# Seven products instead of eight in part of a down projection, and an FFN ordered by a list scheduler

## The chip, the cores and the metric

The kernel runs on one core of a Trainium2 chip. The metric is the device time of one execution in microseconds (us), taken as the median over runs of the same program. The engines are named as in the profile: PE (TensorE) multiplies matrices into eight banks of PSUM, PEld loads its stationary operand, DVE (VectorE) and ACT (ScalarE) do elementwise work and copy banks out, POOL (GpSimd) and SP (SyncE) issue transfers. ACT can issue transfers too.

## The reference

One decoder block on 256 tokens of width 2048, all in float32: a conditioning vector gives six shift, scale and gate vectors (adaLN); a mixed layer (attention and a gated short convolution) comes first; the FFN that the change is about comes last. Cut to that part:

```python
mod = silu(c) @ w_ada + b_ada
sh1, sc1, g1, sh2, sc2, g2 = split(mod, 6)
...
x  = x + g1 * (mixed @ w_out)
h2 = modulate(rms_norm(x, norm2_g), sh2, sc2)
u  = causal_dwconv(h2 @ w_ffn_up, ffn_conv_w, ffn_conv_b)   # 3 taps along the tokens, per channel
u_gate, u_up = split(u, 2)                                  # 5632 channels each
x  = x + g2 * ((silu(u_gate) * u_up) @ w_ffn_down)          # 5632 -> 2048
```

## The kernel before

**Precision.** Each float32 operand `t` of a product is split in two parts for PE: `hi` (ACT copies `t` to the type float32r, L266) and `lo = t - hi` (DVE subtracts, L272). A product is three matmuls: hi by hi, hi by lo, lo by hi. So each loaded weight tile (128 partitions x 4 k-chunks x 512 columns, 1 MB) costs ACT one copy and DVE one subtraction of 128x2048 before PE can use it. Tiles come in six `raw` buffers, `hi` and `lo` have three buffers each. A load starts when `split_lo` has freed a `raw` buffer.

**Slots.** All weight work from the input projection on is one list `slots`; each slot is one weight tile: its load on SP's queue, its split, and a function `go` that issues its matmuls. The main loop walks the list; in turn `i` it issues the split of slot `i + 2` and the matmuls of slot `i`, and between them the small work that `at(i, f)` has put down for that turn. The order on each engine is thus written out by hand: `CFG` holds lags in slots (`up0`, `up`, `gate`, `back`, `slag`, `hi_late` and others), and each engine works through its queue in that order.

**FFN up.** 22 groups of 256 channels. A tile holds 256 gate columns and the 256 up columns that belong to them, loaded as two transfers of 512 KB (L252). Weights are stationary here, the 256 tokens move: per 128x128 block one matmul of 512 columns (tokens' hi and lo side by side, L875) and one of 256 (weight's lo, L878). A group takes four slots (16 k-chunks) and four banks. Six groups are begun on the first eight k-chunks, two slots each (12 slots, called half-turns below), while the rest of the second norm's output is being made, four of them in a form that writes 256 columns only (L861). Then `up_sum` copies the banks out on ACT and adds on DVE, `up_conv` does the three taps (ACT the first with the bias, L734, DVE the two others, L739), `up_silu` and `up_gate` form the gated value and its hi and lo parts `gh`, `gl`.

**FFN down.** The 22 groups are taken in four segments (8, 5, 5 and 4 groups). After a segment's up projection its part of the down projection runs: four column blocks `f` of 512; tokens are stationary (two halves of 128) and weights move, 512 columns per matmul; per k-chunk and `f` there are 2 token halves x 3 matmuls (L433 to L435). Two banks collect a segment for one `f`. `evac_down` sums the segments in eight tiles `dacc` in SBUF. In the last segment `gate_down` multiplies `dacc` by the gate g2 and adds x, which had been parked in the output tensor (`spill`, `unspill`); the last column block has g2 multiplied into its weights instead (L264, `fold`).

**adaLN for g2.** Sixteen tiles of `w_ada` are loaded among the slots and summed on DVE (L330), then spread over the partitions by PE (`spread`).

Of the kernel before, what the change touches and what calls it, by code (L numbers as in the profile page):

```python
# [14 lines left out]
P = 128  # L15
D = 2048
S = 256
# [43 lines left out]
 'slag': [6, 21],  # L61
 'sgap': [2, 6],
# [5 lines left out]
 'up': [[0, 0, 1], [1, 3, 3], [0, 0, 1], [0, 3, 3]],  # L68
 'gate': [-16, -17, -6, -9],
# [17 lines left out]
         'up_conv': 2,  # L87
         'att_p': 0,
# [10 lines left out]
         'gate_down': -1,  # L99
         'conv_g': 2,  # L100
# [9 lines left out]
 'up0': [[0, 2, 4], [0, 3, 3], [0, 2, 2], [0, 1, 2], [2, 2, 4], [2, 4, 6], [0, 1, 2], [0, 0, 5], [3, 4, 4],  # L110
         [0, 2, 3]],
# [5 lines left out]
 'back': [-28, -26, -15, -19],  # L117
# [4 lines left out]
 'hi_late': [5, 8, 12, 14, 15, 16, 17, 18, 19, 20, 21, 23, 27, 28, 35, 39, 40, 45, 49, 53, 56, 58, 61, 65, 66, 67,  # L122
# [12 lines left out]
def tile_block(  # L135
# [11 lines left out]
    sb = ctx.enter_context(tc.tile_pool(name="sb", bufs=1))  # L147
    ps = ctx.enter_context(tc.tile_pool(name="ps", bufs=1, space=bass.MemoryType.PSUM))
# [78 lines left out]

    def load_next():
        if pending:
# [5 lines left out]
            pending.pop(0)(t)  # L235
            ready.append(t)

    def take():
        t = ready.pop(0)
        return t  # L240
# [19 lines left out]
    def split_hi(nk, gate=None):  # L260
        t = take()
        if gate is not None:
            w = t[:, :nk]
            V.tensor_tensor(out=w, in0=w, in1=gB[gate].unsqueeze(1).to_broadcast([P, nk, 512]), op=ALU.mult)  # L264
        hi = sb.tile([P, 4, 512], F32R, tag="hi", bufs=N_HL, name="hi")
        act(hi[:, :nk], t[:, :nk], AF.Copy)  # L266
        halfway.append((t, hi, nk))

    def split_lo():
        t, hi, nk = halfway.pop(0)  # L270
        lo = sb.tile([P, 4, 512], F32R, tag="lo", bufs=N_HL, name="lo")
        V.tensor_tensor(out=lo[:, :nk], in0=t[:, :nk], in1=hi[:, :nk].bitcast(F32), op=ALU.subtract)  # L272
# [11 lines left out]
    class Ada:  # L284
# [30 lines left out]
        def consume(self, r):  # L315
            t = self.view(take())
# [435 lines left out]
    def up_sum(grp, one):  # L752

        new = grp not in ub
        if one:
            if new:
                ub[grp] = [t2k(f"ub{grp}") for _ in range(2)]
            for ft in range(4):
                p, d = zp[grp][ft][:, :256], ub[grp][ft // 2][:, (ft % 2) * 256:(ft % 2) * 256 + 256]
                if new:  # L760
                    act(d, p, AF.Copy)
                else:
                    V.tensor_tensor(out=d, in0=p, in1=d, op=ALU.add)
            del zp[grp]
            return
        c = [t2k(f"ub{grp}") for _ in range(2)]
        for ft in range(4):
            act(c[ft // 2][:, (ft % 2) * 256:(ft % 2) * 256 + 256], zp[grp][ft][:, 256:], AF.Copy)  # L768
# [3 lines left out]
        if new:  # L772
            ub[grp] = c
        else:
            for a, b in zip(ub[grp], c):
                V.tensor_tensor(out=a, in0=a, in1=b, op=ALU.add)
        del zp[grp]

    def up_conv(grp):
        uy[grp] = [t2k(f"uy{grp}") for _ in range(2)]  # L780
        for w in range(2):
            conv3(ub[grp][w], uy[grp][w], fcols[:3], fcols[3], w * 44 + 2 * grp, CFG["taps"][1] if grp < CFG["taps"][2] else 0)
        del ub[grp]

    def up_silu(grp):
        act(uy[grp][0], uy[grp][0], AF.Silu)

    def up_gate(grp):
        g, u = uy.pop(grp)
        V.tensor_tensor(out=g, in0=g, in1=u, op=ALU.mult)  # L790
        hi, lo = t2k(f"gh{grp}", F32R), t2k(f"gl{grp}", F32R)
        act(hi, g, AF.Copy)  # L792
        V.tensor_tensor(out=lo, in0=g, in1=hi.bitcast(F32), op=ALU.subtract)  # L793
# [6 lines left out]
    def fold(seg, f):  # L800
        return seg == len(SEGS) - 1 and f >= CFG["fold"]

    def evac_down(seg, f):
        assert seg < len(SEGS) - 1 or f"gd{f}" in done
        done.add(f"ed{seg}{f}")
        for t in range(2):
            p = mainp["D", seg, f][t]
            if seg == 0:
                dacc[t, f] = t2k(f"da{t}{f}")
                act(dacc[t, f], p, AF.Copy)  # L810
            elif seg < len(SEGS) - 1:
                V.tensor_tensor(out=dacc[t, f], in0=p, in1=dacc[t, f], op=ALU.add)
            else:
                y = t2k(f"d{f}{t}")
                w = 256 if f == 3 and t == 1 else 512
                for h in range(0, 512, w):
                    s = slice(h, h + w)
                    p = mainp["D", seg, f][t + h // 256]
                    if fold(seg, f):
                        V.tensor_tensor(out=y[:, s], in0=p[:, :w], in1=x1[t, f][:, s], op=ALU.add)  # L820
                    else:
                        V.tensor_tensor(out=y[:, s], in0=p[:, :w], in1=gB[G2, f][:, s], op=ALU.mult)
                        V.tensor_tensor(out=y[:, s], in0=y[:, s], in1=x1[t, f][:, s], op=ALU.add)
                    nc.sync.dma_start(rows_of(t, f)[:, s], y[:, s])

    def gate_down(f):
        assert f"ed{len(SEGS) - 2}{f}" in done
# [4 lines left out]

    SEGS, a = [], 0
    for n in CFG["segs"]:
        SEGS.append((a, a + n))
        a += n

    NS, *cut = CFG["split"]
    for seg, (ga, gb_) in enumerate(SEGS):
        turns = [((0, 16), range(ga, gb_))]  # L840
        if seg == 0:
            turns = [(ks, range(NS)) for ks in zip([0] + cut, cut + [16])] + [((0, 16), range(NS, gb_))]
        for n, (ks, grps) in enumerate(turns):
            for grp in grps:
                if seg == 0 and n < len(cut) + 1 and grp < CFG["direct"][min(n, 1)]:
                    direct.setdefault(grp, []).append(ks)
                for k in range(ks[0], ks[1], 4):
                    def go(hi, lo, grp=grp, k=k, ks=ks):
                        if k == ks[0]:
                            zp[grp] = [bank(f"z{grp}_{ft}") for ft in range(4)]  # L850

                        order = [(j, ft) for j in range(4) for ft in range(4)]
                        begins, ends = k == ks[0], k + 4 == ks[1]
                        if grp in direct and ks in direct[grp]:
                            for j in range(4):
                                for ft in range(4):
                                    o, a = zp[grp][ft][:, :256], slice(ft * P, (ft + 1) * P)
                                    for w, v in ((hi, 0), (hi, 1), (lo, 0)):  # L860
# [12 lines left out]
                        for j, ft, w in run:
# [529 lines left out]
```

## Time and profile before

| | before |
|---|---|
| median of 3 runs | 1173.9 us (1173.8 to 1174.57) |
| span of the profiled execution | 1170.4 us |
| PE busy | 1151.1 us |
| DVE busy | 921.9 us |
| ACT busy | 626.3 us |
| POOL busy | 12.0 us |
| moved by DMA | 318.00 MB, mean 272 GB/s |

The three runs shown lie between 1173.8 and 1174.57 us; the profiled execution is told by its span, from the first to the last instruction, 3.5 us under the median of the runs. Busy is the time in which an engine has at least one instruction at work. A matmul's own duration overlaps that of the next, so the pace of matmuls is read from the starts of two that lie far apart. The trace can be cut into stretches: for each, the busy time of every engine, and the matmul clock that the chip granted.

### The profile page before, as it was taken

Reading aid. Unit: us, or ns where it says so; the run is one execution under the profiler, and the core shown is the slowest. Engines: PE = TensorE matmul, PEld = TensorE weight load, DVE = VectorE, ACT = ScalarE, POOL = GpSimd, SP = SyncE. Lnnn points to the kernel's source line nnn. Section 1 sums busy time; section 2 is a strip of 40 time slices with the busy share of each in tenths; the row PEclk is TensorE's granted clock in tenths of the full one; section 3 lists DMA queues with packets and bytes.
Section 4 is the critical chain, followed back from the end, with each engine's and each line's share of the span. In section 5 each row is a group of like instructions: output and inputs, shape, how many; then the busy total and the mean of one; then the engine's idle time right before and its main releaser. Section 6 shows DMA issues by size and latency. Waiting matters only on the chain.

```text
span 1170.4 us, 15668 instructions
## 1 busy us (share of the span) xinstructions
PE 1151.1 (98%) x6115; PEld 973.6 (83%) x6115; DVE 921.9 (79%) x1030; ACT 626.3 (54%) x906; POOL 12.0 (1%) x24
## 2 busy tenths in 40 slices
PE   5999999999999999999999999999999999999998
PEld 3777778888888889988888888888888888888886
DVE  3889989999999978899876767986556576478766
ACT  6645365567785564666664444555444554336441
POOL 1000000000000000000000000000000000000000
PEclk9999999999999999999999999999999999999999
DMA  9999989999899799975555898984664646675441
GB/s 364 406 415 411 409 321 372 378 349 347 287 332 350 251 326 331 359 253 178 186 194 168 305 337 301 310 279 154 208 222 159 201 162 216 222 252 168 150 162 73
DMA packets 189052, 318.00 MB, mean 272 GB/s; under 512 B 7073, under 2 KB 105845, under 8 KB 184625
## 3 DMA queue, kind: packets, MB, share of 16 engines
q1 hardware_dynamic: 187232, 314.60, 75.6%
q10 hardware_dynamic: 1296, 2.16, 0.5%
q8 instruction: 48, 0.79, 0.3%
q0 software_dynamic: 448, 0.24, 0.1%
q14 instruction: 28, 0.22, 0.1%
HBM read 312.77 MB, written 4.19 MB: 271 GB/s over the span
## 4 chain that ended last, share of the span: by engine, by line
PE 91%; DVE 3%; ACT 2%; DMA 2%; issue 1%; SPq 0%; DVEq 0%; ACTq 0%
PE z L875 24%; PE z L878 13%; PE z L861 4%; DVE lo L272 1%; PE ada L324 1%; PE mk L443 1%; PE mk L444 1%; PE mk L441 1%; PE mq L443 1%; PE mq L444 1%; PE mq L441 1%; PE mx L443 1%; PE mc L443 1%; PE mx L444 1%; PE mc L444 1%; PE mv L443 1%
## 5 line engine op out<-in xcount | busy, mean ns | idle before, releaser
L272 DVE TENSOR_TENSOR lo<-raw,hi 128x2048 fp32r<-128x2048 f32 (+2 forms) x201 | 445.9, 2224 | 140.4 <-ACT hi L266 135.5
L266 ACT ACTIVATE hi<-raw 128x2048 fp32r<-128x2048 f32 (+2 forms) x201 | 373.8, 1865 | 311.9 <-PE z L875 60.2
L875 PE MATMUL z<-h,hi 128*128 128x512 f32 x1280 | 299.0, 390 | 0.2 <-DVE h L696 0.2
L875 PEld LDWEIGHTS z<-h,hi 128*128 128x128 f32 x1280 | 237.6, 188 | 48.1 <-PE z L875 0.6
L330 DVE SCALAR_TENSOR_TENSOR ada<-raw,csil,ada 128x512 f32<-128x512 f32 (+3 forms) x167 | 195.4, 1175 | 5.6 <-DMA raw<-in_w_ada_dram 2.1
L878 PEld LDWEIGHTS z<-h,lo 128*128 128x128 f32 x1280 | 159.3, 192 | 3.4
L878 PE MATMUL z<-h,lo 128*128 128x256 f32 x1280 | 160.5, 283 | 0.0
L739 DVE SCALAR_TENSOR_TENSOR uy<-ub,fc,uy 128x254 f32<-128x254 f32 (+1 forms) x176 | 71.3, 476 | 0.2
L771 DVE TENSOR_TENSOR ub<-z,ub 128x256 f32<-128x256 f32 x96 | 33.9, 415 | 37.9 <-ACT ub L768 37.9
L792 ACT ACTIVATE gh<-uy 128x512 fp32r<-128x512 f32 x22 | 13.9, 632 | 62.9 <-DVE uy L790 62.9
L861 PE MATMUL z<-h,hi 128*128 128x256 f32 x256 | 46.6, 284 | 0.4 <-ACT h L693 0.2
L734 ACT ACTIVATE uy<-ub,fc,fc 128x256 f32<-128x256 f32 x88 | 45.6, 602 | 0.0
L768 ACT ACTIVATE ub<-z 128x256 f32<-128x256 f32 x96 | 28.8, 384 | 31.4 <-PE z L875 31.4
L861 PEld LDWEIGHTS z<-h,hi 128*128 128x128 f32 x256 | 40.0, 192 | 0.8 <-ACT h L693 0.5
L861 PE MATMUL z<-h,lo 128*128 128x256 f32 x128 | 36.2, 283 | 0.0
L324 PE MATMUL ada<-raw,crep 128*32 128x256 f32 (+1 forms) x192 | 20.3, 535 | 7.9 <-DMA raw<-in_w_ada_dram 7.9
L793 DVE TENSOR_TENSOR gl<-uy,gh 128x512 fp32r<-128x512 f32 x22 | 15.2, 692 | 15.4 <-ACT gh L792 15.4
L443 PE MATMUL mq<-hi,h 128*128 128x512 f32 x64 | 25.5, 398 | 0.4 <-DVE adaz L361 0.4
L443 PE MATMUL mx<-hi,h 128*128 128x512 f32 x64 | 25.7, 401 | 0.0
L443 PE MATMUL mc<-hi,h 128*128 128x512 f32 x64 | 25.6, 400 | 0.0
L443 PE MATMUL mk<-hi,h 128*128 128x512 f32 x64 | 25.1, 393 | 0.0
L443 PE MATMUL mv<-hi,h 128*128 128x512 f32 x64 | 25.1, 392 | 0.0
(612 smaller groups left out, 1885.4 us busy)
## 6 DMA issues: line engine op xcount, KB each, us to landing
raw<-in_w_ada_dram SPq DMA_DIRECT2D x96, 1024.0 KB, 6.8
raw<-in_w_ffn_up_dram SPq DMA_DIRECT2D x176, 512.0 KB, 4.5
raw<-in_w_in_dram SPq DMA_DIRECT2D x47, 1024.0 KB, 7.8
raw<-in_w_ffn_down_dram SPq DMA_DIRECT2D x28, 1024.0 KB, 5.0
raw<-in_w_out_dram SPq DMA_DIRECT2D x16, 1024.0 KB, 6.0
raw<-in_w_ffn_down_dram SPq DMA_DIRECT2D x20, 768.0 KB, 4.2
xr<-in_x_dram SPq DMA_DIRECT2D x2, 1024.0 KB, 6.4
x<-in_x_dram SPq DMA_DIRECT2D x8, 256.0 KB, 6.6
```

What stands on the lines that cost most here:

```text
L266: act(hi[:, :nk], t[:, :nk], AF.Copy)
L272: V.tensor_tensor(out=lo[:, :nk], in0=t[:, :nk], in1=hi[:, :nk].bitcast(F32), op=ALU.subtract)
L324: mm(self.acc[q:q + 32, :], crep[:, i, :], t[:, j, :], start=(r == 0 and j < 4), stop=(r == self.tiles - 1 and j >= self.rows - 4), tile_p ...
L330: V.scalar_tensor_tensor(out=self.acc, in0=t[:, j, :], scalar=csil[:, i:i + 1], in1=self.acc, op0=ALU.mult, op1=ALU.add)
L443: mm(o, a, hi[:, k, s], start=(first and k == 0), stop=False)
L444: mm(o, b, hi[:, k, s], start=False, stop=False)
L734: act(y[:, s], b[:, s], AF.Identity, bias=bias[:, i + j:i + j + 1], scale=w[2][:, i + j:i + j + 1])
L739: V.scalar_tensor_tensor(out=o[:, d:], in0=v[:, :256 - d], scalar=w[2 - d][:, i + j:i + j + 1], in1=o[:, d:], op0=ALU.mult, op1=ALU.add)
L771: V.tensor_tensor(out=d, in0=zp[grp][ft][:, :256], in1=d, op=ALU.add)
L861: mm(o, w[:, j, a], h2T[k + j][:, v * 256:v * 256 + 256], start=begins and j == 0 and w is hi and not v, stop=ends and j == 3 and w is lo)
L875: mm(zp[grp][ft], hi[:, j, ft * P:(ft + 1) * P], h2T[k + j], start=begins and j == 0, stop=ends and j == 3)
L878: mm(zp[grp][ft][:, :256], lo[:, j, ft * P:(ft + 1) * P], h2T[k + j][:, :256], start=False, stop=False)
```

## The change

It touches the FFN alone, from the first half-turns of the up projection to the end.

1. **Seven products.** Six groups (three in segment 0, two in 1, one in 2; segments are now 8, 6, 4 and 4 groups) are multiplied in the down projection by a Strassen-Winograd scheme. A block is 2 token halves by 2 k-chunks, times 2 k-chunks by 2 column blocks: eight products of 128x128 by 128x512 become seven, each still three matmuls. It needs sums of weights (`sums_of`, three DVE instructions, made in place in the `raw` tile) and sums of tokens (`st_sums`, `st_hi`, `st_lo`). Such a group and column pair takes two slots: `r` (three products, straight from the loaded tile) and `T` (four products, split from the sums, no load of its own). The other groups (`c`) keep eight.
2. **Eight banks and a detour.** Two column blocks are done together, so that a segment and column pair collects in eight banks: four of plain results and four partial products (`a`, `5`, `6`, `7`). `evac_q` copies each out on ACT and POOL adds it to a tensor in DRAM by an accumulating transfer. At the end `load_q` brings the 16 sums back and `join` adds them on DVE. `dacc` and its adds go.
3. **Up projection by half.** A unit is 512 columns of the gate half or of the up half, one transfer of 1 MB, instead of 256 and 256. Two units make two groups. The taps move to ACT: two more scaled copies for each (`utaps` 2), DVE only adds them.
4. **List scheduler.** From the slot after the half-turns on, every piece of work is an `Op` with an engine, a planned cost, what it depends on, a due time and the buffers it needs; a greedy loop emits the piece that can start first, by due time. Every fourth `hi` and `lo` tile now comes from the `raw` buffers, which makes them four deep and leaves four `raw` buffers for loads.
5. **End.** The last segment runs its column blocks in another order (`tail`), with block 3 in the last two slots. Blocks 0 and 1 are added to the output in DRAM by accumulating transfers, blocks 2 and 3 get x by an accumulating transfer into SBUF. The loads for g2 move to the units 9 to 17.

```diff
- 'segs': [8, 5, 5, 4],
+ 'plan': [6, 0, 1, 7, 2, 3, 8, 4, 5, 9, (0, 0), (0, 1), 10, 11, 12, 13, 14, 15, (1, 0), (1, 1), 16, 17, 18, 19, (2, 1), (2, 0), 20, 21],
+ 'tail': [(0,36,4),(1,36,4),(2,36,4),(0,40,4),(1,40,4),(2,40,4),(3,36,4),(3,40,4)],
+ 'utaps': 2,
+ 'segs': [8, 6, 4, 4],
+ 'forms': ['cScScScc', 'cScScc', 'cScc'],
...
+    def half_tile(tag, i):
+        t, n = (tag, N_HL) if i < DEEP or (i - DEEP) % 4 else ("raw", N_RAW)
...
+    def sums_of(t):
+            V.tensor_tensor(out=t[:, 1::2], in0=t[:, 1:3], in1=t[:, 3:4].to_broadcast([P, 2, 512]), op=ALU.add)
+            V.tensor_tensor(out=t[:, 2], in0=t[:, 2], in1=t[:, 1], op=ALU.add)
+            V.tensor_tensor(out=t[:, 0], in0=t[:, 0], in1=t[:, 2], op=ALU.add)
...
+        for d in range(CFG["utaps"] + 1):
+            for j in range(2):
+                if d:
+                    act(z[d - 1][:, s], ub[unit][w][:, s], AF.Copy, scale=fcols[2 - d][:, i:i + 1])
+                else:
+                    act(y[:, s], ub[unit][w][:, s], AF.Identity, bias=fcols[3][:, i:i + 1], scale=fcols[2][:, i:i + 1])
...
+    def evac_q(seg, fp, n):
+            e = t2k(f"e{fp}{n}")
+            act(e, qb.pop((seg, fp, n)), AF.Copy, scale=-1.0 if n in ("a", "c00", "c10") else 1.0)
+            if (fp, n) in qd:
+                nc.gpsimd.dma_start(qd[fp, n], e, accum_op=ALU.add)
+            else:
+                qd[fp, n] = dram.tile([P, 512], F32, name=f"q{fp}{n}")
+                nc.gpsimd.dma_start(qd[fp, n], e)
...
+            if e == "c":
+                todo.append(("c", [(f"c{t}{f}", (tok, j, t), 2 * j + f) for f in range(2) for t in range(2) for j in range(2)], g))
+            else:
+                todo.append(("r", [("a", (tok, *a11), 2), ("c00", (tok, *a12), 0), ("c01", (sT, g, 3), 1)], g))
+                todo.append(("T", [("c10", (tok, *a22), 0), ("7", (sT, g, 1), 1), ("6", (sT, g, 2), 2), ("5", (sT, g, 0), 3)], g))
...
+                    mm(qb[seg, fp, n], y, hi[:, b], start=first[n] == (i, j), stop=False)
+                    mm(qb[seg, fp, n], x, hi[:, b], start=False, stop=False)
+                    mm(qb[seg, fp, n], x, lo[:, b], start=False, stop=last[n] == (i, j))
...
+        for j in ([j] if j < len(slots) else []):
+            d = [pe.get(j - 4)]
+            if kind.get(j) == "T":
+                d.append(sum_op[j - 1])
+            hi_op[j] = prev["hi"] = Op("ACT", 1.81 * nk / 4 + 0.02, lambda j=j: split_hi(slots[j][1], gated.get(j), j), d, key=raw)
+            lo_op[j] = prev["lo"] = Op("DVE", 2.2 * nk / 4 + 0.03, lambda j=j: split_lo(j), [hi_op[j]])
+            if kind.get(j) == "r":
+                sum_op[j] = Op("DVE", 2.4, lambda j=j: sums_of(held[j]), [lo_op[j]])
```

More of the change, by code (lines that the diff above doesn't have):

```diff
@@ L234, in load_next, with arrive, take @@
             t = sb.tile([P, 4, 512], F32, tag="raw", bufs=N_RAW, name="raw")
[L235 to L240, printed above, removed]
+            issue = pending.pop(0)
+            issue(t)
+            ready.append((issue, t))
+            if clock:
+                arrive(issue)
+    clock, landed = {}, {}
+    def arrive(issue):
+        clock["DMA"] = max(clock["DMA"], clock["now"] + 1.5) + 2.7
+        landed[issue] = clock["DMA"] + 1.5
+    def take(issue=None):
+        for e in ready:
+            if issue in (None, e[0]):
+                ready.remove(e)
+                return e[1]
     def w_load(w, k0, nk, cols):
@@ L833, in tile_block @@
+    NS, *cut = CFG["split"]
     SEGS, a = [], 0
@@ L1342, in tile_block, with hi_of, lo_of @@
     at(CFG["vload"] + CFG["fcols"], ffn_cols)
[L1345 to L1347 removed]
+    def hi_of(js):
+        for j in js:
+            split_hi(slots[j][1], gated.get(j), j)
+    def lo_of(js):
+        for j in js:
+            split_lo()
+    for i in range(F0):
+        js = from_(i)
+        if i == F0 - 3:
+            skip.extend((0, 0))
         last = i in CFG["x_first"]
[L1349 to L1350 removed]
+        late = [j for j in js if i == N_OUT or i in CFG["hi_late"]]
+        if not last:
+            hi_of([j for j in js if j not in late])
         now[0] = i
@@ L1355, in tile_block @@
                 f(*a)
-        if more and hi_late and not last:
-            split_hi(slots[i + LA][1], gated.get(i + LA))
-        if more and not last:
-            split_lo()
+        if not last:
+            hi_of(late)
+            lo_of(js)
         for c, f, a in todo:
@@ L1366, in tile_block, with __init__ @@
             g.consume(r)
-        if more and last:
-            split_hi(slots[i + LA][1], gated.get(i + LA))
-            split_lo()
+        if last:
+            for j in js:
+                hi_of([j])
+                lo_of([j])
+    clock.update(PE=0.0, ACT=0.0, DVE=0.0, SP=0.0, POOL=0.0, DMA=0.0, now=0.0)
+    ops = []
+    class Op:
+        def __init__(self, e, cost, f, deps=(), due=1e9, need=(), free=(), lat=0.1, key=None, out=0, nb=0.0):
+            self.e, self.cost, self.f, self.deps, self.due = e, cost, f, [d for d in deps if d], due
+            self.need, self.free, self.lat, self.end, self.key = dict(need), dict(free), lat, None, key
+            self.out, self.nb = out, nb
+            ops.append(self)
@@ new lines, in tile_block, with up_ops @@
+    prev = {}
+    spread_at = {[i for i, g in up_slots if g == e][k]: j for j, (e, k) in enumerate(CFG["spread"])}
+    def up_ops(i):
+        for grp, one, final in ups_at.get(i, []):
+            a = Op("ACT", 1.06, lambda grp=grp, one=one: up_sum_a(grp, one), [pe.get(i)], need={"t": 2}, free={"b": 4} if one else {})
+            if not one:
+                merge = grp in started and final
+                a = Op("DVE", 1.33 + (1.22 if merge else 0), lambda grp=grp: up_sum_v(grp), [a, done_1.get(grp)],
+                       free={"b": 4, "t": 2 if merge else 0})
+            if not final:
+                done_1[grp] = a
+            freeing.append((i, a, 4))
+            if final:
+                chain(grp, a)
@@ new lines, in tile_block, with run_slot @@
+    free = 8
+    q = list(freeing)
+    for i in range(F0, len(slots)):
+        while free < slots[i][4] and q:
+            _, a, n = q.pop(0)
+            a.due = min(a.due, tid[i])
+            free += n
+        free -= slots[i][4]
+    for o in reversed(ops):
+        for d in o.deps:
+            d.due = min(d.due, o.due - o.cost - 0.15)
+    def run_slot(i):
+        now[0] = i
+        for c, f, a in sorted(tasks.pop(i, []), key=lambda e: e[0]):
+            f(*a)
+        if i in spread_at:
+            spread_p[i] = p = bank("adab5")
+            hi, lo = two_g.pop(spread_at[i])
+            mm(p, onesr, hi, start=True, stop=False)
+            mm(p, onesr, lo, start=False, stop=True)
+        slots[i][2](*ready_w.pop(i))
```

559 lines of the change are left out of this document (407 added, 152 removed), and 6 rows, old and new, of the table CFG.

## The prediction

> **What bounds the kernel now.** The page first: share of each engine and the chain that ended last.
>
> ```profile
> span 1170.4 us, 15668 instructions
> PE 1151.1 (98%) x6115; PEld 973.6 (83%) x6115; DVE 921.9 (79%) x1030; ACT 626.3 (54%) x906; POOL 12.0 (1%) x24
> PEclk9999999999999999999999999999999999999999
> PE 91%; DVE 3%; ACT 2%; DMA 2%; issue 1%; SPq 0%; DVEq 0%; ACTq 0%
> ```
>
> PE is busy for 98% at a full clock and makes 91% of the last chain: the kernel is bound by its matmuls. The waits of PE say how little else there is, and the stretches of the FFN (up, down, up, down, up, down, up, end) show where.
>
> ```profile
> engine line waited for: us in total, times, longest us
> PE ada L324 <- DMA raw<-in_w_ada_dram: 7.9, 2, 7.2
> PE pv_ccol L201 <- DMA vcb<-in_c_dram: 4.1, 1, 4.1
> PE m('D', 3, 3)0_9720 L435 <- DVE lo L272: 1.6, 1, 1.6
> ```
>
> ```profile
> core 0: us, PE busy (x) PEld busy (x) DVE busy (x) ACT busy (x) POOL busy (x), PEclk, DMA share, GB/s
> 499.60:610.70 111.10, 111.10 (x640) 98.41 (x641) 97.42 (x140) 69.97 (x97) 0.00 (x0) 1.00 0.62 208
> 610.70:697.90 87.20, 87.20 (x386) 72.23 (x385) 59.03 (x38) 37.94 (x33) 2.31 (x2) 1.00 0.74 264
> 697.90:809.00 111.10, 111.10 (x642) 98.41 (x641) 89.86 (x88) 57.24 (x67) 0.00 (x0) 1.00 0.79 271
> 809.00:864.00 55.00, 55.00 (x244) 45.43 (x243) 33.08 (x34) 24.75 (x25) 0.00 (x0) 1.00 0.60 201
> ...
> 1119.80:1166.30 46.50, 44.75 (x216) 36.80 (x215) 33.44 (x38) 16.74 (x18) 0.00 (x0) 1.00 0.29 108
> ...
> sum 670.80, PE 664.98 PEld 574.63 DVE 480.94 ACT 328.25 POOL 2.31; mean PE 73.89 PEld 63.85 DVE 53.44 ACT 36.47 POOL 0.26
> ```
>
> The long waits lie before the FFN and stay. Inside it PE has no idle time until the last down projection, where 46.50 us hold 44.75 busy: 1.75 us lost, most of it the 1.6 us for the last `lo`. The first row bears on the rest: DVE was at 88% (97.42 of 111.10) there and PE lost nothing. So the change can gain matmuls that go and those 1.75 us, and nothing more; it loses by any wait that it makes.
>
> **Part 1, seven products.** The pace of a 512-column matmul of the down projection comes from two starts of one line, 48 matmuls apart (two slots of 24):
>
> ```profile
> 611.40 0.39 PE L433 MATMUL m('D', 0, 0)1_5607<-hi,gl 128*128 128x512 f32 x1
> 622.28 0.39 PE L433 MATMUL m('D', 0, 0)1_5607<-hi,gl 128*128 128x512 f32 x1
> ```
>
> 10.88 / 48 = 0.227 us. Six groups x 2 column pairs x 1 product x 3 matmuls = 36 matmuls go: **-8.2 us**, all on the path. The shape of the others stays, so does their pace. Slots become uneven: `c` 24 x 0.227 = 5.44, `r` 9 x 0.227 = 2.04, `T` 12 x 0.227 = 2.72 us.
>
> What it adds goes to engines beside PE, priced by busy time over count of the groups by shape:
>
> ```profile
> L272 DVE TENSOR_TENSOR lo<-raw,hi 128x2048 fp32r<-128x2048 f32 x179 | 408.4, 2287 | 107.5 <-ACT hi L266 104.9 <-DMA raw<-in_w_ffn_up_dram 2.5
> L272 DVE TENSOR_TENSOR lo<-raw,hi 128x1536 fp32r<-128x1536 f32 x20 | 35.1, 1757 | 30.6 <-ACT hi L266 28.3 <-PE z L878 2.3
> L272 DVE TENSOR_TENSOR lo<-raw,hi 128x1024 fp32r<-128x1024 f32 x2 | 2.4, 1221 | 2.3 <-ACT hi L266 2.3
> L330 DVE SCALAR_TENSOR_TENSOR ada<-raw,csil,ada 128x2048 f32<-128x2048 f32 x32 | 75.0, 2344 | 0.0
> L739 DVE SCALAR_TENSOR_TENSOR uy<-ub,fc,uy 128x255 f32<-128x255 f32 x88 | 38.4, 476 | 0.2
> L771 DVE TENSOR_TENSOR ub<-z,ub 128x256 f32<-128x256 f32 x96 | 33.9, 415 | 37.9 <-ACT ub L768 37.9
> L776 DVE TENSOR_TENSOR ub<-ub,ub 128x512 f32<-128x512 f32 x12 | 7.7, 681 | 0.0
> L793 DVE TENSOR_TENSOR gl<-uy,gh 128x512 fp32r<-128x512 f32 x22 | 15.2, 692 | 15.4 <-ACT gh L792 15.4
> L746 DVE TENSOR_TENSOR cv<-tap,cv 128x510 f32<-128x510 f32 x4 | 2.7, 682 | 0.0
> L266 ACT ACTIVATE hi<-raw 128x2048 fp32r<-128x2048 f32 x179 | 341.8, 1916 | 261.8 <-PE z L875 55.5 <-DMA raw<-in_w_in_dram 41.6 <-issue 32.7
> L266 ACT ACTIVATE hi<-raw 128x1536 fp32r<-128x1536 f32 x20 | 29.8, 1491 | 45.1 <-issue 10.4 <-PE m('D', 2, 2)1_8599 L434 6.5 <-PE m('D', 1, 2)1_7293 L434 6.5
> L734 ACT ACTIVATE uy<-ub,fc,fc 128x256 f32<-128x256 f32 x88 | 45.6, 602 | 0.0
> L745 ACT ACTIVATE tap<-cp,v1c 128x256 f32<-128x256 f32 x8 | 3.6, 496 | 0.0
> L768 ACT ACTIVATE ub<-z 128x256 f32<-128x256 f32 x96 | 28.8, 384 | 31.4 <-PE z L875 31.4
> L792 ACT ACTIVATE gh<-uy 128x512 fp32r<-128x512 f32 x22 | 13.9, 632 | 62.9 <-DVE uy L790 62.9
> ```
>
> Per seven-product group and pair (12 of them) ACT splits 1.49 + 1.91 instead of 1.91 us, DVE 1.76 + 2.28 instead of 2.28 plus the weight sums, 1.2 + 2 x 0.64 = 2.5. Between two such groups stands one `c` slot, so DVE owes 1.76 + 2.5 + 2.28 + 2.28 = 8.8 us in 10.2 us of PE: 86%, under the 88% above. But there is a chain: `T` is split from sums that wait for `r`'s split. `r` may begin its split when the buffer four slots back is free, and `T` starts four slots later: 2.04 + 2.72 + 5.44 + 2.04 = 12.2 us. In it lie 1.49 + 1.76 + 2.5 + 1.91 + 2.28 = 9.9 us in series, and DVE's 2.28 for the `c` slot between: 12.2 against 12.2, nothing to spare. That holds where a seven-product group follows another after one `c`: twice in each turn of segment 0, once in each of segment 1, six places in all. (The first of a turn has full slots before it, some 18 us.) Each place costs between 0 (the `c` subtraction falls outside the chain) and 2.28 (it lies in it wholly, with another piece of that length ahead). I take 0.4, near the lower end, since the chain just fits by the rows: **+2.4 us**, ends 0 and 13.7.
>
> **Part 2, banks and the detour.** 48 copies of 512 columns on ACT (0.6 each by the L792 row) replace eight copies and 16 adds. POOL issues 48 writes, 16 reads back and 12 transfers for the output, 76 at about half a microsecond by the first row below, 38 us in 660: free, since POOL does nothing else. A copied tile is held until its write has landed, and no accumulating transfer is in the trace:
>
> ```profile
> L310 POOL DMA_DIRECT2D ada<-in_b_ada_dram x2 | 1.0, 504 | 0.6 <-POOL ada L308 0.6
> out_dram<-x ACTq DMA_DIRECT2D x8, 256.0 KB, 6.3
> out_dram<-d SPq DMA_DIRECT2D x7, 256.0 KB, 2.3
> ```
>
> Plain writes of that size land in 2.3 to 6.3 us; with a read added I bound it by twice that, 12.6; the scheduler reserves 9. Cover: a bank's copy is due only when the next turn needs the bank, and `a`, `5`, `6`, `7` end two `c` slots (10.9 us) ahead of it. Cost 0; with the cover gone, rival C. Traffic: 48 tiles of 256 KB written, 32 of them read first, 16 read back, some 25 MB or 38 GB/s more, on stretches that used 0.60 to 0.79 of DMA time for 201 to 271 GB/s: about 0.11 more; hidden.
>
> **Part 3, up units and taps.** PE's slots stay (111.10 / 20 = 5.55 us). ACT gets 8 x 0.45 = 3.6 us a unit, DVE loses 8 x 0.44 - 4 x 0.68 = 0.8. The densest stretch is the first: 28 slots, 155.4 us, ten units. ACT: 28 x 1.91 + 10 x (4 x 0.30 + 4 x 0.52 + 8 x 0.45 + 2 x 0.63) = 53.5 + 81.4 = 135 us, 87% (63% before). DVE: 28 x 2.28 + 10 x (4 x 0.35 + 4 x 0.68 + 2 x 0.69) + 12 x 0.64 + two tiles for g2 at 2.34 + token sums of three groups at an estimated 1.7 (three narrow adds by the L771 row, one `lo` by L793) = 137 us, 88%. Both are as full as DVE was in the first row, at once. The chains of the last units are not due until the down turn is under way, where ACT has room: I take 0; ends 0 and 8.1, one unit's ACT work pushed ahead of a split. Over the whole FFN DVE gets splits 21, weight sums 30, token sums 10, joins 10, less taps 18 and adds 15, so some 520 of 660 us (481 + 38); ACT gets taps 79, splits 18, copies 24, so 450 (328 + 121): neither bounds.
>
> **Parts 4 and 5, order and end.** With four `hi` and `lo` tiles the splits run further ahead. The `at` lags go; that costs nothing itself. At the end block 3's two slots come last, and the gating of their weights no longer stands behind block 2's evacuation: the 1.75 us lost there go, ends -1.75 and +2 (units 20 and 21 finish groups 20 and 21 together, and only three slots, 16.3 us, cover their chain of about 13). I take **-1.7**. What follows the last matmul is the same.
>
> **Sum.** 1170.4 - 8.2 + 2.4 - 1.7 = 1162.9 us of span; the span stands 3.5 under the median of 1173.9, so **1166.4 us**, 7.5 below.
>
> [...]
>
> **Rivals.**
> - A. No new wait: the chain at `T` fits everywhere. 1170.4 - 8.2 - 1.7 + 3.5 = 1164.0. For it: PE at 88% DVE load lost nothing. Against: the chain has no slack.
> - B, the other side. `T` waits for one more subtraction at each of the six places: 1164.0 + 13.7 = 1177.7, slower. It decides from (8.2 + 1.7) / 6 = 1.65 us a place. Against it: 2.28 us at every place needs an order that is wrong each time.
> - C. The accumulating writes land later than 9 us, ACT stands at `evac_q` for a tile, and the splits queued behind it are late: 3 us in each of six turns, 1166.4 + 18 = 1184.
> - D. The first stretch: ACT late by a unit's work, 1166.4 + 8.1 = 1174.5, no change.
> - E. The change doesn't do what it says: the short slots `r` and `T` run no faster than a `c` split can be made, and the 8.2 us become waits for `lo`: 1174.6.
>
> **Chances.** Forecast 0.50 (1164.5 to 1169.5), A 0.20, B 0.10, C 0.05, D 0.10, E 0.05. 0.2% is 2.3 us, about what this measurement can tell from no change: faster means below 1171.6, slower above 1176.2. The forecast, A and a part of D (late by less than a unit) are faster, 0.75; the rest of D, E and a mild B the same, 0.12; B and C slower, 0.13. The range runs from just under A, 1162.5, to 1175, which takes in D and E; with B and C some 0.15 are left out.
>
> **What will show it.** 36 matmuls fewer at 0.227 us. In the waits of PE: `T`'s matmuls for `lo`, at most a few us in all; a total near 10 there is B. No idle PE in the first 155 us after the half-turns; else D. ACT never long idle before an `evac_q` copy; else C. In the last 46 us no wait for the last `lo`. The prediction is wrong if PE's idle time in the FFN grows by more than 5 us, or if the pace of matmuls moves off 0.227.

## The result and the profile after

The changed kernel takes **1166.05 us** (1164.76 to 1167.46), beside 1173.85 us (1172.43 to 1174.57) for the kernel before: ratio 0.9936 [0.9922, 0.995], 7.8 us faster. Predicted were 1166.4, within 1162.5 to 1175. The number is right to 0.4 us, but several of its terms are not; they cancel, and the experiments below are about which. Executions of the kernel before take 1172.2 to 1172.9 us at a mean granted clock of 0.999 to 1.000 or 1173.2 to 1174.7 us at 0.997 to 0.999, and three of these four are of the longer kind: against the median of 1172.6 that the runs beside the experiments gave for it, 1166.05 is 6.5 us faster.

The profiled execution took 1167.0 us with a span of 1165.2. First the page after: engine shares and the chain that ended last.

```profile
span 1165.2 us, 15759 instructions
PE 1143.1 (98%) x6079; PEld 967.0 (83%) x6079; DVE 960.6 (82%) x996; ACT 733.9 (63%) x1134; POOL 68.2 (6%) x100
PE 88%; DMA 7%; DVE 2%; ACT 2%; issue 1%; SPq 0%; DVEq 0%; ACTq 0%
```

PE has 36 matmuls fewer (6115 to 6079) and is busy 8.0 us less. It is still at 98%, so it still sets the time. What is new is in the third row: DMA makes 7% of the last chain instead of 2%. The waits of PE (us in total, times, longest), and the stretches of the FFN that matter (the dense first one, down of segment 0, down of segment 1, the last two up units, the last down), say where:

```profile
PE z L1044 <- ACT ada L1724: 2.1, 1, 2.1
```

```profile
core 0: us, PE busy (x) PEld busy (x) DVE busy (x) ACT busy (x) POOL busy (x), PEclk, DMA share, GB/s
499.40:654.77 155.37, 155.37 (x896) 137.63 (x895) 133.22 (x154) 125.56 (x202) 2.30 (x2) 1.00 0.59 197
654.77:737.73 82.96, 82.96 (x367) 68.72 (x366) 69.83 (x56) 55.01 (x56) 7.86 (x15) 1.00 0.68 245
871.09:934.51 63.42, 63.17 (x278) 51.66 (x276) 48.71 (x42) 42.13 (x47) 10.45 (x12) 1.00 0.81 233
1066.55:1115.96 49.41, 47.31 (x261) 41.19 (x260) 32.77 (x33) 27.57 (x34) 15.29 (x23) 0.97 1.04 331
1115.96:1160.00 44.04, 44.04 (x217) 37.20 (x215) 34.75 (x38) 16.64 (x23) 6.96 (x8) 1.00 0.59 140
```

The wait for the last `lo` of the kernel before is gone: the last down projection has no idle PE (44.04 of 44.04). A new wait stands some 24 us ahead of it, in the last two up units, where the DMA share is 1.04 (packet times added up over the 16 engines; here they come to more than the window) and the granted clock 0.97. In short windows around that wait (same columns):

```profile
1090.00:1092.70 2.70, 0.60 (x3) 0.18 (x1) 2.67 (x5) 2.40 (x2) 0.12 (x1) 1.00 1.05 407
1092.70:1094.00 1.30, 1.29 (x3) 1.11 (x4) 1.30 (x2) 1.19 (x1) 1.30 (x3) 0.53 0.76 293
1094.00:1096.00 2.00, 2.00 (x6) 1.51 (x6) 2.00 (x3) 1.82 (x5) 2.00 (x5) 0.50 0.93 164
```

PE stands for 2.1 us, and then runs for some 3.4 us at about half clock: 13 matmuls take 4.8 us, against 3.3 at the same place in the run with the taps on DVE below, whose clock stays at 1.00. 2.1 idle + 1.7 slow is 3.8 of the 4.0 us by which this stretch is longer than the 45.4 us that two variants below show for it.

What PE waited for, from the chain that ended last, cut to that place, and from the DMA issues between 1037 and 1100 us (count, size of each, median us from issue to landing):

```profile
1057.78 2.30 DVE lo L308
...
1060.10 11.87 DMA raw<-in_w_ffn_up_dram
...
1074.02 2.30 DVE lo L308
...
1076.34 13.84 DMA raw<-in_w_ffn_up_dram
...
1090.26 1.91 ACT hi L299
```

```profile
q1 hardware_dynamic: 5472, 11.90, 53.1%
q0 software_dynamic: 3304, 7.07, 51.2%
...
raw<-in_w_ffn_up_dram SPq DMA_DIRECT2D x8, 1024.0 KB, 12.0
...
q<-e POOLq DMA_DIRECT2D x6, 256.0 KB, 8.8
```

The releaser that the wait names, `ada` L1724, is a copy of 0.58 us right behind this last `hi` on ACT; what held the `hi` was the load. A weight load starts when a `lo` has freed its `raw` buffer, and here takes 11.9 and 13.8 us; between 700 and 870 us the median of the same load was 5.1. In these 63 us POOL's queue (q0) moves 7.07 MB in 51.2% of the DMA time, the weight queue (q1) 11.90 MB in 53.1%: by the byte, POOL's transfers are 1.6 times as dear. All 16 accumulating writes of segment 2 and 13 of the 16 reads back are issued in this window.

Lengths of the stretches of the FFN, from the start of their first matmul to that of the next, in us (segments 1 and 2 have 5 groups each before, and 6 and 4 after, so only down 0 and the last down compare singly with before; the others compare among the variants of the changed kernel):

| | down 0 | down 1 | down 2 | last up units | last down | last matmul ends |
|---|---|---|---|---|---|---|
| before | 87.04 | 54.95 | 54.40 | 88.91 (4) | 46.69 | 1166.3 |
| after | 82.96 | 63.42 | 42.16 | 49.41 | 44.04 | 1160.0 |
| all eight products | 87.04 | 65.28 | 43.52 | 45.44 | 44.04 | 1163.6 |
| no writes of segment 2 | 82.96 | 63.21 | 42.16 | 45.43 | 44.04 | 1155.8 |
| writes of segment 2 twice | 82.96 | 63.11 | 42.16 | 63.17 | 56.56 | 1185.9 |

From before to after the FFN is 6.4 us shorter: products -8.2, last down -2.65, `T`'s `lo` in segment 1 +0.9, last up units +4.0, the rest -0.4. Behind the last matmul 1.1 us come back: 5.2 instead of 4.1 us to the end of the span (the last output tiles on SP's queue land in 3.1 us in the median, 2.3 before; why was not tested). Together -5.2 us, 1170.4 to 1165.2.

### The profile page after: what moved, and what is told of

It is laid out like the page before. It is cut to its first block, busy times and chain, and to the rows that moved or that the text cites. A ratio compares the mean times of both kernels' runs of the same rounds, so it can differ in the third digit from the quotient of the medians.

```text
span 1165.2 us, 15759 instructions
## 1 busy us (share of the span) xinstructions
PE 1143.1 (98%) x6079; PEld 967.0 (83%) x6079; DVE 960.6 (82%) x996; ACT 733.9 (63%) x1134; POOL 68.2 (6%) x100
## 2 busy tenths in 40 slices
DMA packets 140442, 334.76 MB, mean 287 GB/s; under 512 B 6592, under 2 KB 15252, under 8 KB 136016
## 4 chain that ended last, share of the span: by engine, by line
PE 88%; DMA 7%; DVE 2%; ACT 2%; issue 1%; SPq 0%; DVEq 0%; ACTq 0%
PE z L1044 24%; PE z L1047 12%; PE z L1030 4%; PE qc L1008 3%; PE qc L1007 3%; PE qc L1006 3%; DMA raw<-in_w_ffn_up_dram 2%; DMA raw<-in_w_ada_dram 2%; DVE lo L308 1%; DMA raw<-in_w_ffn_down_dram 1%; PE mk L490 1%; PE mk L491 1%; PE mk L488 1%; PE ada L371 1%; PE mq L490 1%; PE mq L491 1%
## 5 line engine op out<-in xcount | busy, mean ns | idle before, releaser
L308 DVE TENSOR_TENSOR lo<-raw,hi 128x2048 fp32r<-128x2048 f32 (+1 forms) x207 | 465.9, 2257 | 107.5 <-ACT hi L299 104.3
L299 ACT ACTIVATE hi<-raw 128x2048 fp32r<-128x2048 f32 (+1 forms) x207 | 390.3, 1892 | 251.6 <-DMA raw<-in_w_ffn_up_dram 60.2
L1008 PE MATMUL qc<-lo,gh 128*128 128x512 f32 x216 | 84.2, 390 | 0.2 <-DVE lo L308 0.2
L1006 PE MATMUL qc<-hi,gl 128*128 128x512 f32 x216 | 84.0, 389 | 0.0
L1007 PE MATMUL qc<-hi,gh 128*128 128x512 f32 x216 | 84.0, 389 | 0.0
L840 ACT ACTIVATE tap<-ub,fc 128x256 f32<-128x256 f32 x176 | 75.0, 505 | 0.0
L856 DVE TENSOR_TENSOR uy<-tap,uy 128x510 f32<-128x510 f32 x88 | 60.2, 687 | 8.3 <-ACT tap L840 3.8
L1008 PEld LDWEIGHTS qc<-lo,gh 128*128 128x128 f32 x216 | 40.6, 188 | 9.4 <-DVE lo L308 1.1
L1007 PEld LDWEIGHTS qc<-hi,gh 128*128 128x128 f32 x216 | 40.6, 188 | 8.4
L1006 PEld LDWEIGHTS qc<-hi,gl 128*128 128x128 f32 x216 | 40.5, 188 | 8.4
```

Of the source, the lines that this page charges most:

```text
L840: act(z[d - 1][:, s], ub[unit][w][:, s], AF.Copy, scale=fcols[2 - d][:, i:i + 1])
L856: V.tensor_tensor(out=pair(y)[:, :, d:], in0=pair(z[d - 1])[:, :, :256 - d], in1=pair(y)[:, :, d:], op=ALU.add)
L1006: mm(qb[seg, fp, n], y, hi[:, b], start=first[n] == (i, j), stop=False)
L1007: mm(qb[seg, fp, n], x, hi[:, b], start=False, stop=False)
L1008: mm(qb[seg, fp, n], x, lo[:, b], start=False, stop=last[n] == (i, j))
```

## The experiments

**Theory** after the result: the products are worth their full 8.2 us; about half of it is given back at the last two up units, since segment 2's detour (copies added to DRAM, and their reading back) fills the DMA queues just there. **Rivals**: the products gain less than 8.2 and the order, the units and the end do the rest; the wait is caused by reading back, not by writing; the wait is one of the ACT or DVE queues in the dense first stretch. Unless named otherwise, an edit is made in the changed kernel.

**All eight products, rest of the change kept.**

```diff
-  'forms': ['cScScScc', 'cScScc', 'cScc'],
+  'forms': ['cccccccc', 'cccccc', 'cccc'],
```


> All six seven-product groups go back to eight products (forms of c alone); scheduler, units, tail and detour through DRAM stay, with four banks a turn instead of eight, so 24 copies and 24 POOL writes instead of 48. Theory 1 (the gain is the 36 matmuls): PE busy in the FFN up by 36 x 0.227 = 8.2 us; since half of the accumulating traffic goes too, the wait of 3.8 us near 1091 us (2.1 idle, 1.7 in slow matmuls after it) shrinks or goes: 1166.05 + 8.2 - 0 to 4.7 = 1169.5 to 1174.3 us. Rival (the gain is the new order, the products only move work): within 1 us of 1166. It also tells what order, units and tail alone are worth against 1173.9.

Measured 1169.38 us (1169.28 to 1170.13), ratio to before 0.9967 [0.9955, 0.998]; span 1167.8. Against the 1172.62 us of the kernel before beside it, the order, the units and the end alone gain 3.2 us. The windows of down 0 and of the last up units:

```profile
655.02:742.06 87.04, 87.04 (x386) 72.12 (x384) 45.46 (x29) 39.80 (x39) 2.73 (x5) 1.00 0.66 215
...
1074.10:1119.54 45.44, 45.44 (x262) 40.12 (x260) 24.80 (x21) 25.52 (x33) 8.35 (x11) 1.00 0.90 265
```

PE is busy in every hundredth. 87.04 - 82.96 = 4.08 = 18 x 0.227 and 43.52 - 42.16 = 1.36 = 6 x 0.227: where the loads are ahead, each matmul that goes shows whole. The products with their detour are then worth 1169.4 - 1166.05 = 3.3 us: 8.2 less the 4.0 and some 0.9 above. 3.2 and 3.3 make the 6.5 us.

**No writes of segment 2.**

```diff
 def evac_q(seg, fp, n):
     e = t2k(f"e{fp}{n}")
     act(e, qb.pop((seg, fp, n)), AF.Copy, ...)
+    if seg == 2:
+        return
```


> Leaves out the 16 accumulating POOL writes of segment 2 (the ACT copies stay), so the output lacks that segment's share. Theory 1 (DMA engines are full at 1045 to 1090 us, each accumulating write of 256 KB takes a read and two moves, and up weights land 12 to 14 us after issue instead of 5): the up loads land in about 5 us, the PE wait near 1091 us goes and with it the slow matmuls: 1166.05 - 3.8 = 1162.3 us, the DMA share there falls from 1.07 to about 0.8. Rival (the loads are late because SP issues them late, behind a buffer that DVE or PE frees): unchanged, 1165 to 1167.

Measured 1162.33 us (1161.77 to 1163.28), ratio 0.9907 [0.9892, 0.9922]; 3.7 us under the changed kernel. The window of the last two up units, and the up loads between 1037 and 1100 us:

```profile
1066.30:1111.73 45.43, 45.43 (x262) 40.11 (x260) 32.80 (x32) 25.54 (x33) 8.03 (x12) 1.00 0.81 260
```

```profile
raw<-in_w_ffn_up_dram SPq DMA_DIRECT2D x8, 1024.0 KB, 7.1
```

The stretch is 4 us shorter and never idle; up loads land in 7.1 instead of 12.0 us (about 5 was expected). For the price of a write the window must hold the same reads in both kernels, and reads move when the writes go. POOL's queue between 1025 and 1115 us, in the changed kernel and here:

```profile
q0 software_dynamic: 4160, 9.44, 44.1%
q0 software_dynamic: 1856, 5.24, 19.8%
```

The difference of 4.20 MB is the 16 writes of 256 KB and nothing else; it took 24.3% of 90 us, 21.9 us of all 16 engines, so **about 1.4 us each**. That it is "a read and two moves" no run shows: the trace counts each such write once. The 16 plain writes of segment 0 in the changed kernel are 4.20 MB too; they took 9.1% of the 115 us from 645 to 760, 0.65 us each. The 16 reads back and 4 additions of x that are left took 17.8 us, 0.9 each. The reads of column pair 1 also come earlier here (1038 to 1056 us instead of 1050 to 1078), so this run alone doesn't separate writes from the reads that stood beside them.

**Reading back later.**

```diff
-  'join': [30.0, 10.0],
+  'join': [30.0, 40.0],
```


> Changes only when the sums of column pair 1 are read back (join 30, 40 instead of 30, 10, so some 30 us later, out of the time of segment 2's writes). Theory 1 with all traffic alike: 8 reads of 256 KB less, about 6 us of DMA time, before 1091 us, so the wait there shrinks to 0 to 2 us: 1163 to 1165 us, unless the reads now delay the last unit's loads. Rival (only the accumulating writes count): unchanged, 1166.

Measured 1170.86 us (1169.63 to 1172.8), ratio 0.9983 [0.9974, 0.9991]. Missed: the wait grew, and a new loss appeared. PE's wait, the first and the last of the 13 reads that POOL issues around it, then the end of the chain that ended last:

```profile
PE z L1044 <- ACT ada L1724: 2.7, 1, 2.7
```

```profile
1073.17 1.57 POOL L923 DMA_DIRECT2D l1a<-q1a  x1
...
1089.15 0.55 POOL L923 DMA_DIRECT2D l0c<-q0c  x1 [0.22 <-issue]
```

```profile
1150.48 0.54 POOL out_dram L967
1151.02 7.17 DMA out_dram<-l0c
```

The edit did not take reads out of the stretch: 13 of the 16 are still issued between 1037 and 1100 us, all of them now between 1073 and 1090, where the changed kernel issues eight between 1050 and 1078 and the next at 1094. The weight load that PE waits for, issued at 1073.1 us, takes 16.9 us among them (13.8 above). The five up loads issued from 1045 to 1067, with writes and no read beside them, take 7.9 to 12.8 us. In the run above, loads with reads alone beside them (1045 to 1057) take 7.3 to 9.1 us, and 4.9 to 5.2 once the reads are over. So both kinds hold up the loads, writes more, and this run doesn't settle which of the two made the wait; the run above, with all reads and none of these writes, has none. The last matmul ends at 1158.9, but the span at 1169.7, 10.8 us later: block 0's addition to the output was pushed behind, and its accumulating transfer ends the kernel. The early reading back is what keeps the end short.

**Two seven-product segments instead of three** (8, 8 and 6 groups; the same six seven-product groups).

```diff
-  'segs': [8, 6, 4, 4],   'forms': ['cScScScc', 'cScScc', 'cScc'],
+  'segs': [8, 8, 6],      'forms': ['cScScScc', 'cScScScc'],
-  'plan': [..., 16, 17, 18, 19, (2, 1), (2, 0), 20, 21],   'join': [30.0, 10.0],
+  'plan': [..., 16, 17, 18, 19, 20, 21],                   'join': [40.0, 80.0],
+  'tail': 12 slots over groups 32 to 43, block 3 last
```


> Segments 8, 8 and 6 groups instead of 8, 6, 4 and 4; three seven-product groups in each of the first two, so still six and still 36 matmuls fewer; 32 bank copies and writes instead of 48 (16 accumulating instead of 32), the tail takes 12 slots. Theory 1 (the waits that remain come from the detour's traffic in short segments): both go, 1166.05 - 3.8 - 0.9 = 1161.4 us, PE waits in the FFN under 1 us. Rival (they come from elsewhere, or the longer tail brings its own): 1165 to 1168.

Measured **1163.23 us** (1163.11 to 1163.53), ratio 0.9914 [0.99, 0.9927]: faster than both kernels, between the two expectations. 16 of the 32 accumulating writes are gone, and the rest land where six up units follow. The window of those units:

```profile
955.25:1091.01 135.76, 135.74 (x778) 119.71 (x776) 103.80 (x105) 87.41 (x127) 16.55 (x24) 1.00 0.85 274
```

PE is full, at a DMA share of 0.85 over these 136 us. It isn't the height of the share that spares PE: from 945 to 970 us it is 1.07 to 1.08 here too. In the changed kernel it stays at 1.04 to 1.08 from 1037 to 1090 us, twice as long, and there the loads fall behind.

**The same two segments with all eight products**, which prices the seven products by themselves.

```diff
-  'forms': ['cScScScc', 'cScScScc'],
+  'forms': ['cccccccc', 'cccccccc'],
```


> The two-segment kernel with eight products in all groups (forms of c alone). No DMA jam in either, so the difference to the two-segment kernel is the seven products alone. Theory 1: 36 x 0.227 = 8.2 us, 1163.2 + 8.2 = 1171.4 us. Rival (part of the 8.2 us is given back as waits for T): 3 to 6 us, 1166 to 1169.

Measured 1169.72 us (1169.46 to 1169.75), so the products bring 1169.7 - 1163.2 = **6.5 us** there, between the two expectations. The down turns give 4.08 (87.04 to 82.96) and 3.56 (87.04 to 83.48), 7.6 of 8.2; the other 0.5, in the second, is `T`'s first product waiting for its `lo` at 890 us (explained further below), so the rival is right in part. The remaining 1.1 us lie in the up stretches (0.8), behind the last matmul (0.2) and ahead of the FFN (0.1), and I did not place them.

**The changed kernel once more**, on the chip of the next three.

> The changed kernel once more, as the measure for the others of this group. If the DMA jam before the last unit varies from run to run, its times spread from about 1164.5 to 1167.5 again, wider than those of the kernel without segment 2's writes (1161.77 to 1163.28).

Measured 1167.53 us (1164.84 to 1168.5), ratio 0.995 [0.9938, 0.9962]. The wait is there again (2.6 us at 1093 us), so it is of the kernel and not of one execution. Its spread, 3.7 us, is some nine times that of the two-segment kernel (0.4): a place that depends on transfers landing in time may be what makes the time vary, but that was not tested.

**Taps back on DVE.**

```diff
-  'utaps': 2,
+  'utaps': 0,
```


> The two further taps go back to DVE (utaps 0: eight multiply-adds of 0.44 us a unit instead of four adds of 0.68; ACT loses 3.6 us a unit). In the first 155 us ACT falls from 87% to about 64%, DVE rises from 88% to about 93%. Theory 1 (the scheduler keeps PE fed as long as no engine is full): unchanged within 1 us. Rival (moving the taps is what lets DVE carry the weight sums): PE waits for lo in the first stretch or the down turns, 2 to 6 us slower.

Measured 1166.28 us (1165.69 to 1167.22): no change. The first stretch:

```profile
499.40:655.00 155.60, 155.60 (x897) 137.80 (x896) 137.81 (x191) 96.51 (x129) 2.31 (x2) 1.00 0.58 196
```

ACT is at 62% and DVE at 89% (93% was expected); in the changed kernel the same stretch (first row of its windows above) has ACT at 81% and DVE at 86%. PE is full in both, so neither engine was near to bounding it. The waits at `T` move, though: down 0 takes 83.52 us instead of 82.96, down 1 62.56 instead of 63.42.

**The old order of the last down projection.**

```diff
-  'tail': [(0,36,4),(1,36,4),(2,36,4),(0,40,4),(1,40,4),(2,40,4),(3,36,4),(3,40,4)],
+  'tail': [(0,36,4),(1,36,4),(0,40,4),(1,40,4),(2,36,4),(3,36,4),(2,40,4),(3,40,4)],
```


> The last segment runs in the order of before, blocks 2 and 3 alternating at the end, all else as changed. Theory 1 (the order alone took away the wait for the last lo): DVE again has block 2's evacuation and the gating between the last splits, 1.7 to 2.7 us slower than the changed kernel. Rival (the scheduler would have hidden it in any order): unchanged.

Measured 1176.36 us (1174.1 to 1179.45), ratio 1.0033 [1.002, 1.0045]; about 9 us worse, more than expected. PE's waits, and DVE before the longer of them:

```profile
PE m('D', 3, 0)0_9820 L480 <- DVE gl L872: 5.7, 1, 5.7
PE z L1044 <- ACT ada L1724: 4.7, 2, 3.8
```

```profile
1123.74 2.28 DVE L308 TENSOR_TENSOR lo<-raw,hi 128x2048 fp32r<-128x2048 f32 x1
1127.62 2.29 DVE L1741 TENSOR_TENSOR raw<-raw,ada 128x2048 f32<-128x2048 f32 x1 [1.60 <-DMA raw<-in_w_ffn_down_dram]
1129.83 2.87 DVE L856 TENSOR_TENSOR uy<-tap,uy 128x510 f32<-128x510 f32 x4
```

In the old order the groups of the last units are needed after two slots (10.9 us), in the new one after three (16.3). Two don't cover their chain: on DVE the gating of a late weight load comes first (L1741, 1.60 us idle before it), with the taps of the last unit behind it, and `gl` comes 5.7 us late. In the profiled execution (1179.06 us) the last down is 8.0 us longer than in that of the changed kernel's repeat, and the last up units are 3.7 us longer.

**The new order of the last down projection in the kernel before.**

```diff
+        if seg == len(SEGS) - 1:
+            parts = [(f, ka + 4 * h, 4) for fs, hs in (((0, 1, 2), (0,)), ((0, 1, 2), (1,)), ((3,), (0, 1))) for h in hs for f in fs]
```


> The kernel before, with only the slots of the last segment in the new order (block 3 alone in the last two slots, all slots of four chunks). Theory 1 (order takes the wait of 1.6 us for the last lo away, by itself): 1.5 to 2.2 us faster than before, 1170.4 to 1171. Rival (it takes the scheduler too, since the lags by hand put the last group's work elsewhere): no faster, or slower by a wait for the last group's gl.

Measured 1175.22 us (1174.21 to 1177.12), ratio 1.002 [1.0011, 1.0028]: slower.

```profile
PE m('D', 3, 0)0_9538 L433 <- DVE gl L793: 3.4, 1, 3.4
```

There the order doesn't help: the wait for the last `lo` goes and one for `gl` of 3.4 us takes its place. The order needs something that the rest of the change brings (the scheduler is the likely part, but units and segments changed with it), and the rest of the change needs the order.

**Every write of segments 0 and 2 done twice**, the second to tensors of its own.

```diff
+                if seg == 2:
+                    nc.gpsimd.dma_start(qx[fp, n], e, accum_op=ALU.add)
...
+                qx[fp, n] = dram.tile([P, 512], F32, name=f"x{fp}{n}")
+                nc.gpsimd.dma_start(qx[fp, n], e)
```


> Each POOL write of segments 0 and 2 is made twice, the second time into a tensor of its own that nobody reads (in segment 2 accumulating too), so 16 more accumulating writes in segment 2. Leaving the 16 out took some 16 us off the time of all 16 DMA engines between 1025 and 1115 us, 1.0 us each. Theory 1 (DMA engines are full there): the up loads come later still and PE waits 8 to 16 us more: 1173 to 1181. Rival (PE waited for something else that the left-out writes happened to free): within 2 us of the changed kernel.

Measured 1192.19 us (1191.13 to 1195.82), ratio 1.017 [1.0155, 1.0184]: 24.7 us over the changed kernel beside it, in the expected direction and larger. PE's waits:

```profile
PE z L1049 <- ACT ada L1729: 11.1, 2, 6.7
PE m('D', 3, 0)0_9868 L480 <- DVE gl L872: 4.0, 1, 4.0
PE m('D', 3, 0)0_9868 L482 <- DVE lo L308: 3.7, 1, 3.7
```

```profile
raw<-in_w_ffn_up_dram SPq DMA_DIRECT2D x8, 1024.0 KB, 17.3
...
q<-e POOLq DMA_DIRECT2D x6, 256.0 KB, 13.2
```

No writes, one set, two sets: the last units take 45.43, 49.41 and 63.17 us, and up loads land in 7.1, 12.0 and 17.3 us (the last over a window of 80 us). The 16 accumulating writes more, some 22 us of traffic at 1.4 each, cost 13.8 us in this stretch and 12.5 in the last down, a part of it at a granted clock of 0.86 and 0.91: 26.3 us in all, with the DMA engines full already (a share of 1.04 to 1.08 in the changed kernel).

**Three seven-product groups in a row in segment 0.** This tests the chain at `T`, with no `c` slot between.

```diff
-  'forms': ['cScScScc', 'cScScc', 'cScc'],
+  'forms': ['ccSSSccc', 'cScScc', 'cScc'],
```


> In segment 0 the three seven-product groups follow one another (ccSSSccc instead of cScScScc), same matmuls. Theory 1 (the prediction's chain r split, weight sums, T split is real but needs more than one c between to be harmless): in a row each such group owes DVE 1.76 + 2.6 + 2.28 = 6.6 us in 4.76 us of PE, so the third is late by about 3.7 us in each of the two turns, PE waits for lo in the down turns of 655 to 738 us, 4 to 8 us more than the changed kernel's 1166 to 1167.5. Rival (the splits run far enough ahead in any order): unchanged.

Measured 1179.35 us (1176.72 to 1183.61), ratio 1.0058 [1.0041, 1.0075]. The down turns of segment 0, and the waits in them:

```profile
654.75:745.46 90.71, 85.75 (x367) 69.56 (x366) 70.17 (x57) 53.74 (x54) 7.02 (x13) 0.98 0.62 219
```

```profile
PE qc L1008 <- DVE lo L308: 3.8, 3, 1.9
PE qc L1006 <- ACT hi L299: 1.3, 1, 1.3
```

90.71 against 82.96 us: +7.75, 5.0 of it idle and the rest mostly a lower clock, at `T` of the third group in each of the two turns, where it was expected (3.7 each). The chain is real; with one `c` slot between, segment 0 of the changed kernel covers it. In all the run is 11.8 us over the changed kernel beside the experiments above, more than expected. The rest of the loss lies mainly at the last up units (52.82 us against 49.92) and was not taken apart.

## Why the prediction was right and where it was wrong

- **Products, -8.2: right**, shown by the down turns of segments 0 and 2 against the eight-product variant, to the hundredth. That PE stays the bound, and that the pace of 0.227 stays, were right too.
- **Waits at `T`, +2.4: right in kind, and nearly three times too large.** At the four places of segment 0 and in segment 2 there is none; rival A was right there. At both places of segment 1 `T`'s first product waits for its `lo`, 0.5 and some 0.35 us, 0.86 in all, where 0.4 each was taken. In the trace of after, PE, then ACT, then DVE at the first of them:

```profile
889.00 0.39 PE L1007 MATMUL qc<-hi,gh 128*128 128x512 f32 x1
889.59 0.50 PE L1008 MATMUL qc<-lo,gh 128*128 128x512 f32 x1 [0.20 <-DVE lo L308]
```

```profile
877.06 1.71 ACT L840 ACTIVATE tap<-ub,fc 128x256 f32<-128x256 f32 x4
878.66 1.48 ACT L299 ACTIVATE hi<-raw 128x1536 fp32r<-128x1536 f32 x1
...
885.24 3.72 ACT L299 ACTIVATE hi<-raw 128x2048 fp32r<-128x2048 f32 x2 [2.77 <-DVE raw L321]
```

```profile
880.18 1.76 DVE L308 TENSOR_TENSOR lo<-raw,hi 128x1536 fp32r<-128x1536 f32 x1 [0.69 <-ACT hi L299]
881.85 0.69 DVE L872 TENSOR_TENSOR gl<-uy,gh 128x512 fp32r<-128x512 f32 x1
882.45 1.22 DVE L319 TENSOR_TENSOR raw<-raw 128x1024 f32<-128x1024 f32 x1
883.71 0.69 DVE L320 TENSOR_TENSOR raw<-raw 128x512 f32<-128x512 f32 x1
884.43 0.69 DVE L321 TENSOR_TENSOR raw<-raw 128x512 f32<-128x512 f32 x1
885.04 6.69 DVE L308 TENSOR_TENSOR lo<-raw,hi 128x2048 fp32r<-128x2048 f32 x3
```

  The pieces last what the rows of before said (1.76, 2.6 for the sums), and the chain is the predicted one: `r`'s split, the sums, `hi` of `T`, `lo` of `T`, 10.9 us in series from 878.7 us. What the prediction didn't have is why it starts late: ACT takes up `r`'s split without a pause behind the taps of the last up unit, which fill it from 873.5 to 878.7 us. With the taps on DVE this wait is gone (down 1 62.56 us), and one of 0.4 us appears at a `T` of segment 0. At the second place a weight load that landed at 914.7 us put the `c` slot's split late, and `T`'s behind it. That 0.4 is near what the two places of segment 1 cost is in part luck: it was a guess on a tie, taken for all six.
- **Detour, 0: wrong, and the largest miss.** The count of 48 writes and 16 reads was right, and so was that they land under 12.6 us (the accumulating ones in 5.1 to 12.4). The step that failed is the average: 25 MB "or 38 GB/s more" over 660 us, "about 0.11 more; hidden". The 25 MB count a read for each of the 32 accumulating writes, which no run shows; the traces count 16.8 MB more (334.76 against 318.00), and what they show of such a write is its time on the engines. The traffic comes in bursts, half of the accumulating writes and most of the reads within 63 us beside two up units and the last weights, and an accumulating write cost the 16 engines 1.4 us there, against 0.9 for POOL's other transfers. Price: 4.0 us by the variant without the writes. Behind the last matmul, too, the variants with less of the detour are shorter (4.2 us with all eight products, 4.8 without the writes, 5.2 after), but why was not tested.
- **Rival C** had the right suspect and the wrong path. ACT doesn't stand at `evac_q` for a tile (2.5 us idle before the 48 copies in all, for PE); the writes hurt through the weight loads beside them, which land in 7.1, 12.0 and 17.3 us with no writes, one set and two. POOL's 16 plain writes of segment 0 are issued in 0.54 to 0.58 us each, while DVE is busy for 84% of that stretch. The full `lo` subtraction on DVE lasts 2288 ns in the mean after and 2287 before, beside 76 issues more on POOL.
- **Last down, -1.7: right in direction, too small** (2.65, of which 1.75 was idle; by the starts of the matmuls before, 2.15 lay at block 3's first ones and 0.4 at 1136 us) **and incomplete in cause.** It is not just that the gating leaves its place behind block 2's evacuation: order alone makes the kernel before slower, and the scheduler with the old order loses 9 us.
- **First stretch, 0 (rival D): right**, PE full with the taps on either engine. **Rival E** is refuted by the down turns.
- **Span to time, +3.5: wrong by 1.7.** After, an execution's own time stands 1.8 us over its span (1167.0 and 1165.2). 3.5 compared one span with a median of other executions; among the runs of the kernel before, those with the same span of 1170.4 take 1172.2 us.

So 1166.4 came out by compensation, and that is luck: 1.5 too much at `T` and 1.7 too much for the offset against 4.0 + 1.1 too little at the last units and behind the last matmul, with -0.9 at the last down and -0.4 in the rest. By signs: -1.5 - 1.7 + 5.1 - 0.9 - 0.4 = 0.6, and this execution took 1167.0, 0.6 over the forecast.

## What to carry to other kernels

Count added traffic for the stretch in which it falls, with an accumulating write at its own price, not as an average over the kernel, and ask how long the queues stay full: 25 us at a DMA share of 1.07 cost PE nothing, 53 us at 1.04 to 1.08 cost it 4 us. Fewer and longer segments make the same saving with half of the accumulating writes. Removed matmuls show to the hundredth where loads and splits run ahead, so compare stretch by stretch against a variant that keeps all the rest; a total that fits can be two errors.

## What the runs showed of the chip

- **The clock after a short idle.** In the profiled execution of the changed kernel 2.1 us of idle PE were followed by some 3.4 us at half clock (0.51 from 1092.7 to 1096.1 us), which nearly doubles the wait's price (2.1 idle and 1.7 slow), and 2.6 us in its repeat were too (its last up units take 49.92 us, 4.5 more than the 45.43 without a wait). At the same place 2.1 us with the taps on DVE and 2.7 us with the later reading back left the clock at 1.00 (13 matmuls in 3.3 us behind each), and so did the 1.6 us of the kernel before, in its last down. So the length of the idle alone doesn't decide it between 2.1 and 2.7 us, and what does these runs don't show.
- **An accumulating write of 256 KB** to DRAM cost about 1.4 us of all 16 DMA engines in the full stretch. The 32 of the changed kernel landed in 5.1 to 12.4 us, 8.6 in the median (medians of 12.8 to 15.9 us for 15 of segment 2's 16 with twice as many), and took POOL 0.84 to 1.87 us to issue. The 16 plain ones landed in 3.6 to 7.5, 6.3 in the median, and took 0.54 to 0.58 to issue.
